# A two-layer hybrid transformer block on one core: the written order at the end of each mixer

## The chip, the cores and the metric

The kernel runs on one core of one Trainium2 chip. The time is the device time of one execution in microseconds (us), taken as the median of several runs. Names used below: TensorE (PE in rows; PEld its weight loads), VectorE (DVE), ScalarE (ACT), GpSimd (POOL) and SyncE (SP), which issues most loads and stores.

## What is computed

The reference runs 2 layers over 512 latent tokens (`x`) and 256 context tokens (`xc`) of width 1024, in fp32. Cut to one layer:

```python
mod = silu(c) @ w_ada[l] + b_ada[l]          # shifts, scales, gates; modc likewise
y, yc = _hybrid_mixer((x * (1 + sc1) + sh1) @ w_in[l], ...)
x = _layer_norm(ALPHA * x + g1 * (y @ w_out[l]), ln1_g[l], ln1_b[l])
x = _layer_norm(ALPHA * x + g2 * _swiglu(x * (1 + sc2) + sh2, w_ffn_in[l], w_ffn_out[l]), ln2_g[l], ln2_b[l])
if not last: ...the same two lines for xc, yc
```

`_hybrid_mixer` is an mLSTM, a differential attention and a grouped-query attention side by side; `_swiglu` is `(silu(u @ W_gate) * (u @ W_up)) @ w_out`. In the last layer only the 512 latent tokens go through the output projection, the norm and the feed-forward.

## The kernel before

**Tokens.** 768 tokens are six tiles of 128: T0, T1 context, T2 to T5 latent. Pairs are groups: 0 is (T0, T1), 1 is (T2, T3), 2 is (T4, T5). Layer 0 has all three at the end of its mixer, layer 1 only 1 and 2.

**Precision.** An fp32 matrix is held as a high and a low half (`wh`, `wl`; `tokh`, `tokl`), the high one a cast on ScalarE, the low one a subtraction on VectorE or POOL. `mm3` (L63) issues three matmuls for one product: high x high, low x high, high x low.

**The end of a mixer** (from L1039) is the output projection with the first layer norm, and the turn of its result into feature layout for the feed-forward. For each token tile T there are three steps:

- `first(c, T)`, c = 2 and 3: 21 matmuls of 256 columns (`pw<-wh,tokh` and so on), then two VectorE operations, L1045 and L1046, that add the result to the residual tile `rs`. (For c = 0 and 1 this was done earlier.)
- `second(T)`: the part of the projection that hangs on the mixer's last outputs, 6 matmuls of 512 columns into two PSUM tiles (`pw<-w`, source name `pw2`; PSUM, the accumulators that TensorE writes), then `finish`: VectorE L1085, L1088, L1089, L1090, L344, a power on POOL (`rstd`, L347), VectorE `nm` (L1156), and four ScalarE operations that normalise `rs` (L1094).
- `third(T)`: `to_feature` transposes the normalised tile on TensorE (8 x 128 columns, L266, `ptx<-ident,rs`, two PSUM tiles of four), ScalarE copies each 128 columns out with scale and bias (`v<-ptx`, L273, 8), casts twice to `tokh` (L275), and VectorE subtracts twice to `tokl` (L276).

`firsts(g)`, `seconds(g)` and `thirds(g)` do a pair of tiles. PSUM before `ps.pool.release()` is the mixer's pool; after it a pool of eight banks (`Banks`), with `pw2` in banks 2 and 3 and `ptx` in 4 and 5, each pair in rotation.

**The feed-forward's beginning.** `FfnA.load(fi)` (L1178) loads the gate and up columns of 128 hidden features and splits them (ScalarE `wh`, L293; VectorE or POOL `wl`, L294; with a pool given, L1192 and L1193). `FfnA.mm(fi, g)` (L1203) is the 48 matmuls of 256 columns of one feature block and one pair: `pc` for pair 0, `pg` and `pu` for the others, each in a bank of its own. Only two feature blocks, fi = 0 and 1, are given inside `mixer`; the rest follow in the feed-forward stage, where VectorE forms token and weight sums (`tf`, `tg`, L1231 to L1241; `S`, `wh`, `wy`, L1272 to L1293) for a scheme with fewer products, and, in layer 0, `aacc` sums of `w_ada` (L203, L205) for layer 1. `store_x1` (L1112) stores the normalised tiles for later.

**What sets the order.** The order is written by hand, but a scheduler of the language moves an instruction to another place in its engine's queue within what data and buffers allow; each engine then runs its queue in that order, and a waiting instruction holds all behind it.

Of the kernel before, what the change touches and what calls it, by code (L numbers as in the profile page):

```python
# [48 lines left out]
def kernel(ctx: ExitStack, tc: tile.TileContext, a: dict, out: bass.AP):  # L49
# [15 lines left out]
    def mm3(out, sh, sl, mh, ml, first, last):  # L65
        mm(out, sh, mh, first, False)
        mm(out, sh, ml, False, False)
        return mm(out, sl, mh, False, last)
# [188 lines left out]
    def tok_tiles(groups):  # L257
        return [{g: x[:, :, g * 256:(g + 1) * 256] for g in groups} for x in tokhl]
# [124 lines left out]
    def mixer(l, xh, xl, yd, ps, fill, pre):  # L383
        last = l == DEPTH - 1
# [7 lines left out]
        def pool(name, **kw):  # L392
            return tc.alloc_tile_pool(name=f"{name}{l}", reuse_waits="tile", **kw)
# [554 lines left out]
        ps = MixPS(f"psm{l}", acc=("acc", "pv"), q=("acc", "pv"))  # L948
# [18 lines left out]
        boost, fw, aw, pw, ow = MERGE[l]  # L967
# [4 lines left out]
        at = pool("at", bufs=2)  # L972
# [14 lines left out]
        groups = [1, 2] if last else [0, 1, 2]  # L987
# [49 lines left out]
        def first(c, T):  # L1037
            g, o = T // 2, (T % 2) * P
            cs = slice(c * 256, (c + 1) * 256)  # L1039
            wh, wl = W[c]  # L1040
            po = ps.tile([P, 512], F32, tag=("acc", "t")[T % 2], name="pw")[:, 0:256]
            for k in (0, 1, 6, 7, 2, 3, 4):
                mm3(po, Y[0][g][:, k, o:o + P], Y[1][g][:, k, o:o + P], wh[:, k, 0:256], wl[:, k, 0:256], k == 0, k == 4)
            r = R[c, T // 3][:, T % 3]
            V.tensor_tensor(po, po, rows["g1"][1 if T < 2 else 0][:, cs], ALU.mult)  # L1045
            V.scalar_tensor_tensor(r, r, ALPHA, po, ALU.mult, ALU.add)  # L1046
# [6 lines left out]
        xh, xl = {}, {}  # L1053

        anchor = [None]
        fa = FfnA(l)
# [12 lines left out]
        two = {"pw": pair, "tx": lambda: ps.tile([P, 512], F32, tag="t", name="ptx")}  # L1069

        def second(T):
            g, o = T // 2, (T % 2) * P
            pw = two["pw"]()
            for hf in range(2):
                mm3(pw[hf], yh[g][:, 5, o:o + P], yl[g][:, 5, o:o + P], w5[0][hf], w5[1][hf], True, True)
            with tc.issue_after(anchor[0].ins) if anchor[0] is not None else nullcontext():
                finish(T, pw)
# [18 lines left out]
        def third(T):  # L1096
            s, g = 1 if T < 2 else 0, T // 2
            if g not in xh:
                nh, nl = tok_tiles([g])
                xh.update(nh)  # L1100
                xl.update(nl)
            to_feature(lambda kk: R[kk // 2, T // 3][:, T % 3, (kk % 2) * P:(kk % 2) * P + P], T, xh, xl,
                       cols[(l, "ffn", s)], two["tx"],
                       lambda: at.tile([P, 4, P], F32, tag="og", name="v", bufs=3))
# [9 lines left out]
        def firsts(g):  # L1114
            for c in (2, 3):
                for T in (2 * g, 2 * g + 1):
                    first(c, T)

        def seconds(g):
            for T in (2 * g, 2 * g + 1):  # L1120
                second(T)

        def thirds(g):
            for T in (2 * g, 2 * g + 1):
                third(T)

        end = groups[-1]
        firsts(groups[0])
        for g in groups[1:]:
            if g == end:  # L1130
                fa.load(0, at)
            firsts(g)
            seconds(g - 1)
            thirds(g - 1)
        ps.pool.release()
        ps = fa.ps = Banks(f"psg{l}")
        two.update(pw=lambda: [ps.turn_of((2, 3), "pw2") for _ in range(2)], tx=lambda: ps.turn_of((4, 5), "ptx"))
        seconds(end)
        fa.load(1)
        for g in groups[:-1]:  # L1140
            fa.mm(0, g, xh, xl)
        thirds(end)
        fa.mm(0, end, xh, xl)
        for g in groups[:-1]:
            fa.mm(1, g, xh, xl)
        for i in range(2):
            store_x1(i)
        rows["pool"].release()
# [356 lines left out]
    ps = Banks("psm")  # L1505
# [5 lines left out]
    xh, xl = tok_tiles([0, 1, 2])  # L1511
# [82 lines left out]
    for l in range(DEPTH):  # L1594
        yd = tc.dram_tile([2, KD, P, NTOK], F32R, name=f"yd{l}")
        fill = [(0, 1), (0, 2)] if l == 0 else []
        xh, xl, ps, fa = mixer(l, xh, xl, yd, ps, fill, pre)
        nxt, pre, ps = ffn(l, xh, xl, ps, fa)
        if nxt:
            xh, xl = nxt  # L1600
# [37 lines left out]
```

## Time and profile before

| | |
|---|---|
| Time, median of 3 runs | 2044.14 us (2041.57 to 2046.82) |
| The profiled execution | 2053.77 us, its span 2052.0 us |
| Mean granted TensorE clock | 0.954 |
| TensorE matmul | 1905.9 us busy (93%), 12424 instructions |
| VectorE | 1369.3 us (67%) |
| ScalarE | 852.1 us (42%) |
| POOL | 341.5 us (17%) |
| Chain that ended last | TensorE 69%, VectorE 17%, DMA 5%, ScalarE 5% |

Over the span TensorE is the busiest engine by far, but its matmuls overlap and their ends are modelled, so 93% isn't a measure of how much could be won; what counts is where it stands still or runs at half clock. The ends of the two mixers lie at about 610 to 660 us (layer 0) and 1660 to 1705 us (layer 1).

### The profile page before, as it was taken

The numbers are of one execution on the slowest core, as the hardware profiler recorded it, in microseconds if no ns is written. First come the engines' busy times: TensorE is split into PE (matmuls) and PEld (weight loads), VectorE is DVE, ScalarE is ACT, GpSimd is POOL, SyncE is SP. The second block draws the span as 40 slices with busy tenths as digits, with TensorE's granted clock in tenths as the row PEclk, the third lists the DMA queues.
The fourth block names the chain that finished last, engine by engine and source line by source line (L and its number), as shares of the span: only waits on it lengthen the run. The fifth ranks groups of instructions, "written<-read, shape, count | busy, mean of one in ns | idle before, by whom it ended". The sixth has DMA issues, their size and how long they took to land.

```text
span 2052.0 us, 31613 instructions
## 1 busy us (share of the span) xinstructions
PE 1905.9 (93%) x12424; PEld 1695.6 (83%) x12424; DVE 1369.3 (67%) x2526; ACT 852.1 (42%) x1605; POOL 341.5 (17%) x287
## 2 busy tenths in 40 slices
PE   7889799999998999999699998879999989999998
PEld 5778767778987999999587788878889879999886
DVE  3556645576566999975556765755575578888746
ACT  4334355344346333433234433335553354444430
POOL 0223200112220000000301211421012610000301
PEclk9998899999998999999899999889999889999999
DMA  8211252226314446743665630121114333333431
GB/s 293 64 45 37 68 158 68 94 77 190 103 53 144 134 147 197 220 135 103 222 217 173 185 129 24 42 62 31 42 32 108 95 96 101 90 99 104 176 122 62
DMA packets 213232, 233.09 MB, mean 114 GB/s; under 512 B 14096, under 2 KB 185506, under 8 KB 213082
## 3 DMA queue, kind: packets, MB, share of 16 engines
q1 hardware_dynamic: 203034, 214.28, 33.6%
q0 software_dynamic: 10048, 16.78, 3.0%
q8 instruction: 98, 1.61, 0.3%
q14 instruction: 52, 0.43, 0.1%
HBM read 204.77 MB, written 26.25 MB: 113 GB/s over the span
## 4 chain that ended last, share of the span: by engine, by line
PE 69%; DVE 17%; DMA 5%; ACT 5%; issue 4%; SPq 1%; POOL 0%; DVEq 0%; ACTq 0%; POOLq 0%
PE po L63 18%; PE pacc L63 13%; PE px L1301 7%; PE pw L63 5%; PE pyz L1301 5%; PE s L63 5%; PE pv L63 3%; DMA raw<-w_ffn_in 3%; PE ppt L839 2%; DVE ca L455 2%; PE pg L63 1%; PE pu L63 1%; DMA araw<-w_ada 1%; DVE wl L1272 1%; PE pa L175 1%
## 5 line engine op out<-in xcount | busy, mean ns | idle before, releaser
L63 PE MATMUL po<-wh,tokh 128*128 128x256 f32 (+1 forms) x832 | 254.0, 305 | 10.7 <-DVE VG L418 3.5
L63 PE MATMUL po<-wh,tokl 128*128 128x256 f32 (+1 forms) x832 | 246.0, 296 | 0.0
L63 PE MATMUL po<-wl,tokh 128*128 128x256 f32 (+1 forms) x832 | 245.6, 295 | 0.0
L294 POOL TENSOR_TENSOR wl<-raw,wh 128x1024 fp32r<-128x1024 f32 x56 | 135.8, 2445 | 439.0 <-ACT wh L293 346.4
L63 PE MATMUL pacc<-wh,hh 128*128 128x512 f32 x440 | 173.9, 403 | 16.2 <-ACT hh L1434 15.2
L63 PEld LDWEIGHTS po<-wh,tokh 128*128 128x128 f32 x832 | 169.5, 204 | 21.5 <-issue 6.9
L63 PE MATMUL pacc<-wl,hh 128*128 128x512 f32 x440 | 176.1, 401 | 3.0 <-DVE wl L307 3.0
L63 PE MATMUL pacc<-wh,hl 128*128 128x512 f32 x440 | 172.2, 398 | 0.0
L63 PEld LDWEIGHTS po<-wl,tokh 128*128 128x128 f32 x832 | 169.8, 204 | 1.2 <-issue 0.2
L63 PEld LDWEIGHTS po<-wh,tokl 128*128 128x128 f32 x832 | 168.9, 203 | 1.1 <-issue 0.5
L826 DVE TENSOR_REDUCE mx<-s 128x1 f32<-128x768 f32 (+1 forms) x120 | 100.9, 848 | 48.0 <-PE s L63 47.5
L828 ACT ACTIVATE e<-s,mx 128x768 f32<-128x768 f32 (+1 forms) x120 | 98.0, 819 | 78.8 <-DVE mx L826 58.3
L63 PEld LDWEIGHTS pacc<-wh,hh 128*128 128x128 f32 x440 | 84.3, 192 | 39.1 <-ACT hh L1434 17.0
L307 DVE TENSOR_TENSOR wl<-raw,wh 128x1024 fp32r<-128x1024 f32 x66 | 97.9, 1515 | 25.8 <-ACT wh L306 25.6
L347 POOL TENSOR_TENSOR rstd<-rstd,nhalf 128x4 f32<-128x4 f32 (+2 forms) x52 | 43.5, 839 | 377.9 <-DVE rstd L344 324.4
L63 PEld LDWEIGHTS pacc<-wl,hh 128*128 128x128 f32 x440 | 83.9, 191 | 23.9 <-DVE wl L307 3.7
L418 DVE TENSOR_TENSOR pl<-ppt,ph 128x512 fp32r<-128x512 f32 (+1 forms) x112 | 71.9, 650 | 47.2 <-ACT ph L417 46.9
L63 PEld LDWEIGHTS pacc<-wh,hl 128*128 128x128 f32 x440 | 83.3, 189 | 20.1
L293 ACT CAST wh<-raw 128x1024 fp32r<-128x1024 f32 x70 | 70.6, 1051 | 62.4 <-issue 19.4
L417 ACT CAST ph<-ppt 128x512 fp32r<-128x512 f32 (+1 forms) x112 | 61.4, 558 | 77.4 <-PE ppt L839 73.3
L63 PE MATMUL s<-KA,QA 64*128 64x256 f32 (+1 forms) x432 | 86.6, 369 | 5.5 <-ACT e L828 4.0
L63 PEld LDWEIGHTS s<-KA,QA 64*128 64x128 f32 x432 | 62.6, 196 | 30.6 <-ACT e L828 10.9
(444 smaller groups left out, 5428.0 us busy)
## 6 DMA issues: line engine op xcount, KB each, us to landing
raw<-w_ffn_in SPq DMA_DIRECT2D x176, 256.0 KB
araw<-w_ada SPq DMA_DIRECT2D x80, 512.0 KB
raw<-w_ffn_out SPq DMA_DIRECT2D x66, 512.0 KB
raw<-w_in SPq DMA_DIRECT2D x32, 512.0 KB
raw<-w_out SPq DMA_DIRECT2D x18, 512.0 KB
hd<-th POOLq DMA_DIRECT2D x22, 384.0 KB, 3.5
hr<-hd SPq DMA_DIRECT2D x22, 384.0 KB
araw<-w_ada SPq DMA_DIRECT2D x32, 256.0 KB
```

The lines of the kernel that those rows point to most:

```text
L63: return TE.matmul(out, lhsT, rhs, start=start, stop=stop)
L293: S.copy(h, raw[:, :, 0:n])
L294: wsub[0].tensor_tensor(wl[:, 4 * hf:4 * hf + 4, 0:n], raw[:, :, 0:n], f32(h), op=ALU.subtract)
L307: V.tensor_tensor(wl[:, i * wide:(i + 1) * wide], raw[:, 0:wide], f32(h), ALU.subtract)
L347: last_pow[0] = G.tensor_tensor(r, r, nhalf[:, 0:n], op=ALU.pow)
L417: S.copy(dh, src)
L418: V.tensor_tensor(dl, src, f32(dh), ALU.subtract)
L455: V.scalar_tensor_tensor(ca[:, b0:b0 + n], cr[:, b0 + t:b0 + t + n], cw[:, l, fi, t:t + 1], ca[:, b0:b0 + n], ALU.mult, ALU.add)
L826: V.tensor_reduce(mx, s[:, 0:nk], AX.X, ALU.min)
L828: S.activation(e[:, 0:nk], s[:, 0:nk], AF.Exp, bias=mx, scale=-1.0, accum_out=su)
L839: TE.transpose(pt[:, i * P:(i + 1) * P], e[:, kt * P:(kt + 1) * P], ident)
L1301: TE.matmul(po, w[:, u, k], x[v][:, k], start=start and k + i == 0, stop=stop and k == 3 and i == 2, skip_group_check=True)
```

## The change

The loop at the end of `mixer` is replaced by two orders written out, one for each layer; the switch to the `Banks` pool becomes a function `to_banks`. In layer 0 all projections are given first, broken by the `seconds` and `thirds` of pair 0; `seconds` of pair 1 comes after the switch of pools; `mm` of pairs 0 and 1 is given between the `thirds`. In layer 1 the `seconds` of pair 1 are given before the projections of the last pair, and the `seconds` of the last pair before the `thirds` of pair 1; both `mm` of pair 1 come ahead of the last `thirds`.

```diff
--- before.py
+++ after.py
@@ -1124,25 +1124,46 @@
             for T in (2 * g, 2 * g + 1):
                 third(T)
 
+        def to_banks():
+            nonlocal ps
+            ps.pool.release()
+            ps = fa.ps = Banks(f"psg{l}")
+            two.update(pw=lambda: [ps.turn_of((2, 3), "pw2") for _ in range(2)], tx=lambda: ps.turn_of((4, 5), "ptx"))
+
         end = groups[-1]
         firsts(groups[0])
-        for g in groups[1:]:
-            if g == end:
-                fa.load(0, at)
-            firsts(g)
-            seconds(g - 1)
-            thirds(g - 1)
-        ps.pool.release()
-        ps = fa.ps = Banks(f"psg{l}")
-        two.update(pw=lambda: [ps.turn_of((2, 3), "pw2") for _ in range(2)], tx=lambda: ps.turn_of((4, 5), "ptx"))
-        seconds(end)
-        fa.load(1)
-        for g in groups[:-1]:
-            fa.mm(0, g, xh, xl)
-        thirds(end)
-        fa.mm(0, end, xh, xl)
-        for g in groups[:-1]:
-            fa.mm(1, g, xh, xl)
+        if last:
+            seconds(groups[0])
+            fa.load(0, at)
+            firsts(end)
+            to_banks()
+            seconds(end)
+            thirds(groups[0])
+            fa.load(1)
+            fa.mm(0, 1, xh, xl)
+            fa.mm(1, 1, xh, xl)
+            thirds(end)
+            fa.mm(0, end, xh, xl)
+        else:
+            firsts(1)
+            seconds(0)
+            fa.load(0, at)
+            for T in (4, 5):
+                first(2, T)
+            thirds(0)
+            for T in (4, 5):
+                first(3, T)
+            to_banks()
+            seconds(1)
+            fa.mm(0, 0, xh, xl)
+            thirds(1)
+            fa.load(1)
+            seconds(end)
+            fa.mm(0, 1, xh, xl)
+            fa.mm(1, 0, xh, xl)
+            thirds(end)
+            fa.mm(1, 1, xh, xl)
+            fa.mm(0, end, xh, xl)
         for i in range(2):
             store_x1(i)
         rows["pool"].release()
```

What the scheduler makes of it, at three places.

ScalarE in layer 0, where pair 0's copies out of the transposes begin (`v<-ptx`, with the per-feature scale and bias `col_ffn`; `rs` is a normalise, `wh<-raw` a weight cast). Before:

```order
L273 ACTIVATE v<-ptx,col_ffn_5638 128x128 x4
L275 CAST tokh<-v 128x4x128
L273 ACTIVATE v<-ptx,col_ffn_5638 128x128 x8
L1094 ACTIVATE rs<-rs,nm,rstd 128x256 x4
L275 CAST tokh<-v 128x4x128
L273 ACTIVATE v<-ptx,col_ffn_5638 128x128 x4
L275 CAST tokh<-v 128x4x128
L293 CAST wh<-raw 128x1024 x2
L1094 ACTIVATE rs<-rs,nm,rstd 128x256 x4
```

Changed:

```order
L293 CAST wh<-raw 128x1024 x2
L273 ACTIVATE v<-ptx,col_ffn_5638 128x128 x8
L275 CAST tokh<-v 128x4x128
L273 ACTIVATE v<-ptx,col_ffn_5638 128x128 x4
L275 CAST tokh<-v 128x4x128
L273 ACTIVATE v<-ptx,col_ffn_5638 128x128 x4
L275 CAST tokh<-v 128x4x128 x2
L293 CAST wh<-raw 128x1024 x2
L1094 ACTIVATE rs<-rs,nm,rstd 128x256 x4
```

The two weight casts that stood between T1's copies and the next normalise now stand ahead of all copies.

TensorE in layer 0 at the end of the projections and pair 1's transposes (`pw<-wh` projection; `pw_...<-w_...` the six wide matmuls of a `second`). Before, from T5's last projection to T4's `second`:

```order
L63 MATMUL pw<-wh,tokl 128x256
L266 MATMUL ptx<-ident,rs 128x128 x16
L63 MATMUL pw_6845<-w_6311,tokh 128x512
L63 MATMUL pw_6845<-w_6313,tokh 128x512
L63 MATMUL pw_6845<-w_6311,tokl 128x512
L63 MATMUL pw_6846<-w_6312,tokh 128x512
L63 MATMUL pw_6846<-w_6314,tokh 128x512
L63 MATMUL pw_6846<-w_6312,tokl 128x512
L63 MATMUL pc<-tokh,w_6619 128x256
```

Changed, from T5's `second` to the first `pg` of pair 1:

```order
L63 MATMUL pw_6939<-w_6314,tokh 128x512
L63 MATMUL pw_6939<-w_6312,tokl 128x512
L266 MATMUL ptx<-ident,rs 128x128 x8
L63 MATMUL pg<-tokh,w_6571 128x256
L63 MATMUL pu<-tokh,w_6571 128x256
L63 MATMUL pg<-tokh,wh 128x256
L63 MATMUL pu<-tokh,wh 128x256
L266 MATMUL ptx<-ident,rs 128x128 x2
```

T3's eight transposes now stand behind both `second`s of pair 2 and directly ahead of the first `pg` and `pu` of its pair; before, both tiles' sixteen stood together ahead of those `second`s.

TensorE in layer 1. Before, from the last projection to the first `pg`:

```order
L63 MATMUL pw<-wh,tokl 128x256
L266 MATMUL ptx<-ident,rs 128x128 x16
L63 MATMUL pw_16536<-w_16204,tokh 128x512
L63 MATMUL pw_16536<-w_16206,tokh 128x512
L63 MATMUL pw_16536<-w_16204,tokl 128x512
L63 MATMUL pw_16537<-w_16205,tokh 128x512
L63 MATMUL pw_16537<-w_16207,tokh 128x512
L63 MATMUL pw_16537<-w_16205,tokl 128x512
L63 MATMUL pg<-tokh,w_16310 128x256
```

Changed, from the last matmul of T4's `second` (its other five stand directly ahead) to the first `pg`:

```order
L63 MATMUL pw_16491<-w_16207,tokl 128x512
L266 MATMUL ptx<-ident,rs 128x128 x8
L63 MATMUL pw_16520<-w_16206,tokh 128x512
L63 MATMUL pw_16520<-w_16208,tokh 128x512
L63 MATMUL pw_16520<-w_16206,tokl 128x512
L63 MATMUL pw_16521<-w_16207,tokh 128x512
L63 MATMUL pw_16521<-w_16209,tokh 128x512
L63 MATMUL pw_16521<-w_16207,tokl 128x512
L266 MATMUL ptx<-ident,rs 128x128 x12
L63 MATMUL pg<-tokh,w_16370 128x256
L63 MATMUL pu<-tokh,w_16370 128x256
L63 MATMUL pg<-tokh,wh 128x256
```

T4's `second` now stands ahead of T2's transposes and T5's between T2's and T3's; four transposes of T4 have come ahead of the first `pg`.

## Rows read from the trace of the kernel before

**Rows 1.** Stretch, us, busy PE, PEld, DVE, ACT, POOL, clock, DMA, GB/s; layer 0.
```profile
610.00:620.00 10.00, 8.10 (x52) 7.30 (x51) 8.74 (x26) 8.81 (x23) 1.08 (x2) 0.87 0.14 44
620.00:630.00 10.00, 6.32 (x44) 5.44 (x42) 7.45 (x12) 10.00 (x21) 0.00 (x0) 0.84 0.73 224
630.00:640.00 10.00, 6.44 (x31) 5.46 (x32) 6.86 (x14) 5.65 (x15) 0.00 (x0) 0.61 0.34 100
```

**Rows 2.** TensorE's waits, 610 to 645 us: in total, times, longest.
```profile
PE ptx L266 <- ACT v L273: 4.0, 3, 1.6
PE pw L63 <- ACT v L273: 3.4, 2, 2.7
PE ptx L266 <- DVE rs L1046: 1.7, 1, 1.7
```

**Rows 3.** TensorE timeline, layer 0: start, duration, instruction, [idle before].
```profile
619.02 0.41 PE L63 MATMUL pw<-wl,tokh 128*128 128x256 f32 x1
619.23 0.41 PE L63 MATMUL pw<-wh,tokl 128*128 128x256 f32 x1
...
637.40 0.41 PE L63 MATMUL pc<-tokh,w 128*128 128x256 f32 x1
```

**Rows 4.** Chain that ended last, 640 to 750 us: start, duration, piece.
```profile
642.45 2.38 PE pc L63 x20
...
650.52 0.87 PE ptx L266 x8
...
659.96 0.75 DVE aacc L203
...
747.00 2.38 PE px L1301 x12
```

**Rows 5.** VectorE timeline before the `aacc` sums, layer 0.
```profile
658.68 0.69 DVE L276 TENSOR_TENSOR tokl<-v,tokh 128x512 fp32r<-128x512 f32 x1 [2.94 <-ACT tokh L275]
659.29 1.41 DVE L203 TENSOR_SCALAR aacc<-araw,cT 128x1024 f32<-128x1024 f32 x2
```

**Rows 6.** TensorE timeline, layer 0, first wait after the plain matmuls.
```profile
715.59 0.41 PE L1301 MATMUL pyz<-t0h,wh 128*128 128x384 f32 x1 [3.75 <-DVE th L1387]
```

**Rows 7.** ScalarE timeline, layer 0.
```profile
621.63 2.01 ACT L293 CAST wh<-raw 128x1024 fp32r<-128x1024 f32 x2
...
659.04 0.62 ACT L275 CAST tokh<-v 128x512 fp32r<-128x512 f32 x1
```

**Rows 8.** The same stretches view for layer 1.
```profile
1660.00:1670.00 10.00, 7.20 (x58) 6.74 (x56) 9.44 (x22) 4.53 (x6) 1.47 (x1) 0.93 0.19 54
1670.00:1680.00 10.00, 4.37 (x16) 2.54 (x15) 5.83 (x14) 9.69 (x24) 0.56 (x1) 0.50 0.71 209
...
1700.00:1710.00 10.00, 10.00 (x87) 10.00 (x86) 9.97 (x11) 3.69 (x5) 0.00 (x0) 1.00 0.00 0
```

**Rows 9.** TensorE's waits, 1660 to 1705 us.
```profile
PE ptx L266 <- ACT rs L1094: 6.3, 2, 3.5
PE ptx L266 <- DVE rs L1046: 1.4, 1, 1.4
```

**Rows 10.** ScalarE timeline, layer 1.
```profile
1668.52 2.08 ACT L1094 ACTIVATE rs<-rs,nm,rstd 128x256 f32<-128x256 f32 x4 [1.02 <-DVE nm L1156]
...
1671.48 2.90 ACT L273 ACTIVATE v<-ptx,col_ffn 128x128 f32<-128x128 f32 x8
1674.24 1.16 ACT L275 CAST tokh<-v 128x512 fp32r<-128x512 f32 x2
```

**Rows 11.** VectorE timeline, layer 1, last projection.
```profile
1671.17 0.42 DVE L1046 SCALAR_TENSOR_TENSOR rs<-rs,pw 128x256 f32<-128x256 f32 x1
```

**Rows 12.** TensorE timeline, layer 1.
```profile
1669.17 1.18 PE L266 MATMUL ptx<-ident,rs 128*128 128x128 f32 x4 [2.80 <-ACT rs L1094]
...
1682.07 0.38 PE L63 MATMUL pg<-tokh,w 128*128 128x256 f32 x1
...
1698.09 0.39 PE L63 MATMUL pg<-tokh,wh 128*128 128x256 f32 x1 [1.16 <-ACT v L273]
```

## The prediction

> **What bounds the kernel now.** I read the table of engine time by stretches first, around the end of each mixer, then TensorE's waits there, then the rows of ScalarE and VectorE that end them, and last the chain of work that ended last, to see whether time lost there is lost to the program.
>
> Layer 0: from 610 to 640 us TensorE is busy 8.10, 6.32 and 6.44 of each 10 us and its granted clock is 0.87, 0.84 and 0.61 [rows 1]; on both sides it is at 10.00 and 1.00. Its waits sum to 4.0 + 3.4 + 1.7 = 9.1 us, all for copies out of PSUM on ScalarE (`v`) and VectorE [rows 2]. A 256-column matmul starts every 0.21 us there at half clock (619.02 to 619.23) [rows 3], against 2.38/20 = 0.119 us at full clock [rows 4]. The work between 612 and 637.40 us, where the first feed-forward matmul stands [rows 3], is 42 projection matmuls (5.0 us at 0.119), 12 of twice the width (2.9) and some 32 transposes (0.87/8 = 0.11 each [rows 4], 3.5), so about 11.4 us in 25.4: 14 us are lost, 9.1 in waits and 5 to the clock.
>
> After that TensorE has plain work and VectorE takes over: the chain runs on VectorE with the `aacc` sums from 659.96 us on and is back on TensorE at 747.00 [rows 4]. The sums stand behind the last `tokl` of tokens T4 and T5: VectorE had idled 2.94 us for T5's first `tokh` cast, and begins `aacc` at 659.29 [rows 5]. TensorE then waits 3.75 us for VectorE's `th` at 715.59 [rows 6]. So in layer 0 it is not the 14 us that count but **when the `tokh` of T5 is cast** (659.04 [rows 7]).
>
> Layer 1: TensorE is busy 7.20 and 4.37 of 10 us from 1660 to 1680, at clock 0.93 and 0.50, and from 1700 on 10.00 at clock 1.00 [rows 8]. Waits: 6.3 + 1.4 us at the transposes [rows 9] and 1.16 at a `pg` [rows 12]. As TensorE is full behind it, what is lost here is lost to the program.
>
> **The change part by part.** No instruction is added or dropped; only the order, PSUM banks and waits move. 0.3% (about what a measurement of this kernel can tell from no change) is 6.1 us. Durations are those of the profiled execution, 2053.77 us with a span of 2052.0; the median of the runs shown is 2044.14, 0.47% below, and the sum is put on that median.
>
> *SyncE and POOL.* The loads of `w_ffn_in` no longer queue behind the four `x1d` stores, and POOL's and VectorE's splits of them follow. No wait of TensorE in either stage ends on a load [rows 2, 9, 12], so I cost it at nothing; the cover is ScalarE's work ahead of the casts. Were it gone, a load would cost at most the wait it ends, none of which is here.
>
> *Layer 0, first half.* All projections but those of the last tile (21 matmuls) now come ahead of the first transposes, which start at about 613.0. ScalarE's order puts two `wh` casts ahead of T0's `v` groups; the pair costs 2.01 us [rows 7]. So `v` starts at 615.15, and 16 of them (2.76 per 8 [rows 10]) with three casts of 0.55 end at 621.7. TensorE holds both `ptx` banks until the third group of four is read, so the last 21 projection matmuls start at 619.85 and, at 0.21 falling to 0.119, end at 623.8. The pair T2's `pw2` follows (to 626.3), then 47 matmuls of mm(0, 0), 5.6 us, to 631.9. Before, these began at 637.4 [rows 3]; this is the gain that the change makes here.
>
> *Layer 0, second half.* It pays for that with T2 and T3: their norm ran beside the first half, and now begins only after all projections. T2's normalise comes at 633.7. From there ScalarE has for four tokens 4 x 2.0 (normalise) + 4 x 2.76 (`v`) + 8 x 0.55 = 23.4 us [rows 10], so it cannot end before 657.1, and it waits on the way: about 2 us for T2's transposes, and again where T3's come only after T4's and T5's `pw2` (642.8 to 643.6). The first `pg` needs the `tokh` of T3, which I lay at 647.15: TensorE waits 3.55 us with nothing else ahead of it in its order. I let the clock fall there, as it did in [rows 1] after waits of this size on the same copies: 15 matmuls at 0.21 in place of 0.119, 1.5 us. Then come 50 matmuls (7.4 us with those 15), T4's eight transposes, 30 matmuls, T5's transposes with nine more between, ending at 660.9, and one `v` group and cast: the last `tokh` at 663.7 against 659.04 [rows 7], `aacc` at 663.4 against 659.29. That is +4.1 us on VectorE's chain. TensorE has by then done 185 plain matmuls instead of 135 and ends its plain part some 2 us sooner, where it then waits longer for VectorE [rows 6]; a part of VectorE's queue (weights, `w_ada` sums) doesn't hang on the tokens. I take **+3.0**, with ends 0 (VectorE makes up all of it) and +4.1 (nothing).
>
> The Trainium skill's "TensorE: Matmul & The Clock Gate", section "Loop structure matters more than you think", names the copy out of PSUM as work that doesn't break the clock's warmth, and long waits for loads as what does. The rows speak against it: there is no wait for a load here and the clock is 0.61 [rows 1, 2]. By the page the clock terms of both layers would be nil, and the sum +3.4 in place of +6.5.
>
> *Layer 1.* Same until 1666.4. Then TensorE's order puts T4's `pw2` ahead of T2's transposes. Its second half waits for VectorE's `rs` at L1046 of the last projection (1671.17 [rows 11]), so T2's transposes start at 1673.0; before, they waited only for ScalarE's normalise of T2 and started at 1669.17 [rows 12]. T5's `pw2` waits for VectorE as well. ScalarE then has T2's eight `v`, T3's normalise (2.0), T3's `v`, T4's normalise put before T3's casts, and the second cast ends about 1685.1; the first `pg` starts there. Before, the first `pg` stood at 1682.07 [rows 12], so +3.0, of which 1.8 us is paid back, since T4's and T5's `pw2` and four transposes are done by then; the half clock of the longer stretch takes 1.6 back. T4's and T5's transposes come later too, behind two more waits for `v`, and the `pg` that waited 1.16 us at 1698.09 [rows 12] comes at about 1701.5: **+3.5**, carried on, as TensorE is full behind it. Ends: 0 (all paid back) and +6 (none of the work done early helps).
>
> **Sum:** +3.0 + 3.5 = +6.5 us: the profiled 2053.77 would become 2060.3, and the median 2044.14 becomes 2050.6. With the ends of the two terms, 2044 to 2054.
>
> **The rivals.**
> 1. *Clock holds.* If TensorE's clock stays full in the new stretches, 1.5 and 1.6 us fall away: +3.4, 2047.5, no change. For it: more work stands on end, 47 and 50 matmuls against 42 before. Against it: 0.61 and 0.50 with the same waits [rows 1, 8].
> 2. *ScalarE is fed without a gap (the other side).* The place is ScalarE from T2's normalise to T5's last cast. In layer 1 that took from 1668.52 to 1700.5, 32 us, for 23.4 + 1.0 (one `wh` cast) of work, so 7.5 us are idle. If the feed-forward matmuls cover every wait, the end comes 7.5 us sooner there, and 2 us sooner in layer 0 (657.1 against 659.04): -9.5, 2034.6, faster. The point that decides: the 6.1 us are reached when, beside the 2 us of layer 0, layer 1 gives 4.1, so when ScalarE's idle time there falls below 7.5 - 4.1 = 3.4 us. For it: TensorE's waits of 6.3 us for a normalise [rows 9] are at places where other matmuls now stand. The Trainium skill's "Perfetto Trace Analysis", section "Matmuls", asks for just that, independent groups rotating through banks so that reading one out overlaps the next; no row shows yet that it does here. Against it: the new order's own waits above.
> 3. *Hidden in layer 0.* The `aacc` sums wait for loads of `w_ada` and absorb the whole +4.1; then only layer 1 counts: +3.5, 2047.6, no change. It also covers the case that the scheduler's order leaves the stage as long as it was.
> 4. *Half clock all through.* If TensorE stays at half clock from 619 to 647 and from 1670 to 1701, the roughly 100 and 40 matmuls there cost 0.09 more each: 12.6 on top of 3.4, of which some third falls in waits, so +12, 2056.
>
> **How the numbers follow.** The forecast 0.42, and it straddles the bound at 6.1: 0.25 slower, 0.17 no change. Rivals 1 and 3 together 0.18: 0.14 no change, 0.02 on either side. Rival 2, 0.30: half of it lies by its full price, 0.26 faster and 0.04 no change. Rival 4, 0.10, slower. Sums: faster 0.28, no change 0.35, slower 0.37. Range: from 2034 (rival 2 in full) to 2058 (rival 4 and a little), with no more than 2 in 10 left out; the forecast's own is 2044 to 2054.
>
> **What would show it.** Right: in layer 0 a wait of TensorE of 3 to 4 us before the first `pg`, after T3's transposes; feed-forward `pc` matmuls by 627 us; `aacc` begun at 662 to 664; two `wh` casts before the first `v`. In layer 1 the first `pg` at about 1685, after T4's and T5's `pw2`, and that stage's end, where TensorE is at 10.00 again, later by 3 to 4 us. Wrong: `aacc` before 659, ScalarE without gaps from T2's normalise to T5's cast, or TensorE at clock 1.00 through both stages.

## The result: slower by 0.5%, and the profile after

The changed kernel takes 2058.73 us (median of 7 runs, 2053.51 to 2064.82) beside 2046.11 us of the kernel before on the same chip: ratio 1.0052, interval 1.0034 to 1.0070, so +10.6 us (+7 to +14; the two medians alone lie 12.6 apart). Its profiled execution took 2059.73 us, 1.0 above its median; that of the kernel before lay some 8 us above the median of these runs. So stages are compared from an instruction ahead of the change on, not by whole executions. A "shift" below is how much later an instruction starts than its twin before, less the shift at `prs`, a TensorE instruction ahead of the stage.

TensorE's timeline before: the mark ahead of layer 0's stage, and a matmul of the output half of the feed-forward behind it.

```profile
597.04 0.95 PE L63 MATMUL prs<-ones,sq 128*128 128x2 f32 x8
...
1008.17 0.79 PE L63 MATMUL pacc<-wh,hh 128*128 128x512 f32 x1 [15.24 <-ACT hh L1434]
```

The same two after:

```profile
592.86 0.95 PE L63 MATMUL prs<-ones,sq 128*128 128x2 f32 x8
...
1011.48 0.79 PE L63 MATMUL pacc<-wh,hh 128*128 128x512 f32 x1 [14.97 <-ACT hh L1455]
```

The first starts 4.2 us sooner than before and the second 3.3 later: layer 0's stage, read this way, has grown by **7.5 us**. The same reading in layer 1 (from `prs` at 1655 to the first `px` of the feed-forward) gives +6.0. In kernels of the experiments that leave a stage as it was, it shows 0.0 to -0.7 for layer 0, but +0.8 to +1.9 for layer 1. So it is good to 1 us in layer 0, and in layer 1 it stands 1 to 2 us too high: +0.8 to +1.9 there is no change, and the +6.0 is some 4 to 5.

Engines by stretches after (columns as in [rows 1]), which answer to [rows 1] and [rows 8]:

```profile
610.00:620.00 10.00, 6.78 (x33) 5.77 (x33) 5.03 (x6) 8.71 (x22) 0.00 (x0) 0.66 0.36 105
620.00:630.00 10.00, 9.02 (x65) 8.31 (x64) 8.40 (x19) 2.00 (x2) 0.54 (x1) 1.00 0.36 107
630.00:640.00 10.00, 10.00 (x75) 9.32 (x74) 9.26 (x26) 7.70 (x18) 0.54 (x1) 1.00 0.48 157
640.00:650.00 10.00, 6.63 (x44) 6.29 (x42) 5.84 (x18) 8.11 (x19) 1.83 (x3) 0.83 0.19 62
...
1670.00:1680.00 10.00, 5.50 (x15) 3.89 (x16) 9.79 (x25) 7.52 (x17) 0.56 (x1) 0.55 0.85 249
1680.00:1690.00 10.00, 6.56 (x29) 5.16 (x29) 6.78 (x20) 9.35 (x24) 1.10 (x2) 0.67 0.01 2
...
1700.00:1710.00 10.00, 8.11 (x54) 7.63 (x53) 4.28 (x6) 6.35 (x16) 0.00 (x0) 0.83 0.01 2
```

In layer 0 the hole of the stretch 620 to 640 is closed, as meant; the one at 610 is deeper (6.78 where 8.10 stood) and a new one stands at 640. In layer 1 the stretch from 1700 on, which was at 10.00 and clock 1.00, has fallen to 8.11 and 0.83.

TensorE's waits after, 605 to 750 us and, from the fifth line on, 1655 to 1715 us (total, times, longest), for [rows 2, 9]:

```profile
PE px L1322 <- ACT ab L1340: 6.0, 1, 6.0
PE pg L63 <- ACT tokh L275: 3.4, 1, 3.4
PE ptx L266 <- ACT v L273: 2.4, 2, 1.8
PE pu L63 <- DVE wl L294: 1.9, 1, 1.9
...
PE pw L63 <- DVE rs L1046: 4.6, 1, 4.6
PE ptx L266 <- ACT rs L1094: 2.3, 1, 2.3
```

The short waits at the transposes of layer 0 have shrunk from 9.1 us (with `pw`) to about 5, but two long ones follow: 3.4 us before the first `pg`, and 6.0 where 3.75 stood [rows 6]. The 1.9 us for a weight split (`wl`) fall at 683.69, behind the stage, and are new too. TensorE's timeline at those places, and at the last wait of layer 1 (which answers to the one at 1698.09, [rows 12]):

```profile
643.61 0.58 PE L63 MATMUL pg<-tokh,w 128*128 128x256 f32 x1 [3.37 <-ACT tokh L275]
643.99 0.41 PE L63 MATMUL pu<-tokh,w 128*128 128x256 f32 x1
644.20 0.41 PE L63 MATMUL pg<-tokh,wh 128*128 128x256 f32 x1
...
720.07 0.69 PE L1322 MATMUL px<-t1h,wh 128*128 128x384 f32 x1 [6.02 <-ACT ab L1340]
...
1686.73 0.58 PE L63 MATMUL pg<-tokh,w 128*128 128x256 f32 x1 [1.15 <-ACT tokh L275]
...
1702.62 0.66 PE L266 MATMUL ptx<-ident,rs 128*128 128x128 f32 x4 [1.16 <-ACT v L273]
1704.01 0.39 PE L63 MATMUL pg<-tokh,wh 128*128 128x256 f32 x1 [0.74 <-ACT v L273]
```

ScalarE after, layer 0's last cast [rows 7], and the idle time ahead of T4's copies, in layer 0 and then in layer 1:

```profile
630.04 2.08 ACT L1094 ACTIVATE rs<-rs,nm,rstd 128x256 f32<-128x256 f32 x4 [7.73 <-DVE nm L1177]
...
651.83 2.90 ACT L273 ACTIVATE v<-ptx,col_ffn 128x128 f32<-128x128 f32 x8 [3.13 <-PE ptx L266]
...
659.86 0.62 ACT L275 CAST tokh<-v 128x512 fp32r<-128x512 f32 x1
...
1701.06 2.90 ACT L273 ACTIVATE v<-ptx,col_ffn 128x128 f32<-128x128 f32 x8 [8.96 <-PE ptx L266]
```

VectorE before, where the `aacc` sums catch up with their loads, some microseconds behind [rows 5]:

```profile
667.72 1.28 DVE L205 SCALAR_TENSOR_TENSOR aacc<-araw,cT,aacc 128x1024 f32<-128x1024 f32 x1 [0.53 <-DMA araw<-w_ada]
668.92 1.75 DVE L1231 TENSOR_TENSOR tf<-tokh 128x1536 f32<-128x1536 f32 x1
```

And after, with the start of the sums:

```profile
660.11 1.41 DVE L203 TENSOR_SCALAR aacc<-araw,cT 128x1024 f32<-128x1024 f32 x2
...
670.17 1.28 DVE L205 SCALAR_TENSOR_TENSOR aacc<-araw,cT,aacc 128x1024 f32<-128x1024 f32 x1 [2.27 <-DMA araw<-w_ada]
671.37 1.75 DVE L1252 TENSOR_TENSOR tf<-tokh 128x1536 f32<-128x1536 f32 x1
```

With the 4.18 us of the mark added, `aacc` begins at 664.29 against 659.29: +5.0. The load of `w_ada` is then waited for 2.27 us where it was 0.53, and the token sum `tf` comes at 675.55 against 668.92: **+6.6**. VectorE made nothing up; it lost more. TensorE's long wait in the feed-forward, which ends on this chain, grew from 3.75 to 6.02 us.

### The profile page after: what moved, and what is told of

Read it like the earlier page. It is cut to its first block, busy times and chain, and to the rows that moved or that the text cites. A ratio compares the mean times of both kernels' runs of the same rounds, so it can differ in the third digit from the quotient of the medians.

```text
span 2058.0 us, 31619 instructions
## 1 busy us (share of the span) xinstructions
PE 1908.1 (93%) x12424; PEld 1695.3 (82%) x12424; DVE 1366.0 (66%) x2526; ACT 849.7 (41%) x1605; POOL 341.1 (17%) x287
## 4 chain that ended last, share of the span: by engine, by line
PE 71%; DVE 15%; DMA 6%; ACT 4%; issue 3%; SPq 0%; POOL 0%; DVEq 0%; ACTq 0%; POOLq 0%
PE po L63 17%; PE pacc L63 13%; PE px L1322 9%; PE pyz L1322 6%; PE pw L63 5%; PE s L63 5%; PE pv L63 3%; DMA raw<-w_ffn_in 3%; PE ppt L839 2%; DVE ca L455 2%; PE pg L63 2%; PE pu L63 1%; DMA araw<-w_ada 1%; PE pa L175 1%; DVE wl L1293 1%
```

## The experiments

Eleven kernels ran, on three chips, each in several rounds beside the kernel before on the same chip. Layer 0's order and layer 1's can be set apart, so each edit goes into one layer and the other keeps the order of before, unless said. Shifts in us, read as above; "cast" is the last `tokh` cast of T5 in layer 0; times are (ratio - 1) x 2046 us. The ratios aren't quotients of the medians; these would give -7.7 us in the last row.

| kernel | cast | layer 0 | layer 1 | time | ratio, interval |
|---|---|---|---|---|---|
| the change | +5.0 | +7.5 | +6.0 | +10.6 | 1.0052 (1.0034 to 1.0070) |
| layer 0 of it alone | +5.2 | +7.7 | - | +8.0 | 1.0039 (1.0024 to 1.0054) |
| layer 1 of it alone | - | 0.0 | +5.2 | +3.7 | 1.0018 (1.0005 to 1.0032) |
| layer 0, last transposes sooner | +1.7 | +2.7 | - | +6.8 | 1.0033 (1.0016 to 1.0049) |
| layer 1, T2's transposes first | - | -0.7 | +6.2 | +4.1 | 1.0020 (1.0005 to 1.0035) |
| layer 1, last transposes sooner | - | -0.4 | +1.9 | -0.6 | 0.9997 (0.9978 to 1.0016) |
| before, all `second`s sooner | +0.7 | -0.2 | - | +0.8 | 1.0004 (0.9987 to 1.0022) |
| before, splits on POOL | +1.8 | +1.2 | +3.2 | +6.1 | 1.0030 (1.0007 to 1.0053) |
| combined, splits on POOL | -1.3 | -1.1 | +0.9 | -3.7 | 0.9982 (0.9966 to 0.9998) |
| before, layer 0's cast late | +6.5 | +6.2 | +1.2 | +2.9 | 1.0014 (0.9996 to 1.0033) |
| before, banks first in layer 0 | -5.6 | -6.9 | +1.9 | -5.7 | 0.9972 (0.9956 to 0.9988) |
| combined, without POOL | -5.6 | -6.8 | +0.9 | -9.6 | 0.9953 (0.9934 to 0.9971) |

### One layer at a time

Layer 0's branch as in the change, with the loop of before in the other (the diff, cut, is against the change); and the reverse.

```diff
         if last:
-            seconds(groups[0])
...
+            for g in groups[1:]:
...
```

> The new order in layer 0 only; layer 1 as before. Theory (VectorE's chain of sums starts later because the last token's cast is later, and TensorE waits for it after its plain work): about +6 us against the kernel before (+4.5 to +8), some two thirds of the whole change. Rival (only layer 1 counts, since layer 0's stage is hidden behind the w_ada loads): within 2 us of before.

> The new order in layer 1 only; layer 0 as before. Theory (TensorE is full behind the stage, so its later first and second pg blocks are carried to the end): +3.5 to +5 us against the kernel before. Rival (the matmuls done ahead pay it back by the end of the plain part): within 2 us.

Measured +8.0 and +3.7; together 11.7 against 10.6 for both. So the loss is two losses, and layer 0's is the larger, by their middles about two to one (+5 to +11 and +1 to +7).

### Layer 0: the last pair's transposes sooner

```diff
             seconds(end)
+            thirds(end)
             fa.mm(0, 1, xh, xl)
             fa.mm(1, 0, xh, xl)
-            thirds(end)
             fa.mm(1, 1, xh, xl)
```

> Layer 0 of the change with the last pair's transposes given ahead of the feed-forward columns of pairs 1 and 0 (two lines exchanged); layer 1 as before. Theory (the time of T5's last cast decides, not TensorE's waits in the stage): T5's last cast some 5 us sooner than in the run with layer 0 alone, the aacc sums begun as much sooner, and the time 3 to 6 us below that run, so near the kernel before. Rival (what counts is TensorE's time lost in the stage): TensorE waits more for copies, since less work stands between the transposes, and the time is the same as or above the run with layer 0 alone.

T5's cast came 3.5 us sooner than in layer 0's run (+1.7 against +5.2) and the stage 5 us sooner by the profile, but the times moved from +8.0 to +6.8 only, with intervals that overlap widely. TensorE's other waits up to that stage's end stayed: 3.38 us before the first `pg`, at 648.68, and clock 0.83 from 645 to 655, as in the change. So in the profile 5 us of the stage went with the cast and not with that wait. The profiled execution paid 1.66 us later, in the output half (TensorE's timeline of this kernel):

```profile
1033.17 0.51 PE L63 MATMUL pacc<-wl,hh 128*128 128x512 f32 x1 [1.66 <-DVE wl L307]
```

That is not enough to make up the difference. By its time this run doesn't confirm that the late cast is the loss.

### Layer 1: T2's transposes ahead of the last pair's seconds

```diff
             to_banks()
+            thirds(groups[0])
             seconds(end)
-            thirds(groups[0])
             fa.load(1)
```

> Layer 1 of the change with the transposes of pair 1 given ahead of the second of the last pair (two lines exchanged); layer 0 as before. Theory (T4's second, waiting for VectorE's last projection step, holds T2's transposes back by about 4 us): T2's transposes start at their old place, and the time is 3 to 4 us below the run with layer 1 alone, within 1.5 us of the kernel before. Rival (the loss comes from the switch of banks and from the order of ScalarE's copies): no gain over the run with layer 1 alone.

No gain over layer 1's order alone (+4.1 against +3.7). TensorE's timeline of this kernel (its `prs` mark 6.5 us sooner than before):

```profile
1663.05 1.18 PE L266 MATMUL ptx<-ident,rs 128*128 128x128 f32 x4 [3.13 <-ACT rs L1094]
...
1675.31 0.39 PE L63 MATMUL pg<-tokh,w 128*128 128x256 f32 x1 [1.35 <-ACT tokh L275]
...
1692.94 0.66 PE L266 MATMUL ptx<-ident,rs 128*128 128x128 f32 x4 [1.16 <-ACT v L273]
1694.33 0.66 PE L266 MATMUL ptx<-ident,rs 128*128 128x128 f32 x4 [0.74 <-ACT v L273]
1696.24 0.58 PE L63 MATMUL pg<-tokh,wh 128*128 128x256 f32 x1 [1.26 <-ACT v L273]
```

T2's transposes are back at their old time (1663.05 + 6.5 = 1669.6 against 1669.17, [rows 12]) and the first `pg` at 1681.8 against 1682.07. Yet the stage is as late as in the change, for its end has three waits, 1.16 + 0.74 + 1.26 us, at the last pair's transposes, with half clock behind them. The order of T2's transposes is not the cause; the profile shows this for the place alone; the times, with their intervals, could hide a gain of some 3 us.

### Layer 1: the last pair's transposes sooner

From that came a new theory: the change gives all 96 matmuls of pair 1 first, so that the last sixteen transposes are given together behind them (in the change's trace ten of them stand there, in the last run's all sixteen), with nothing to run while ScalarE copies.

```diff
             fa.mm(0, 1, xh, xl)
+            thirds(end)
             fa.mm(1, 1, xh, xl)
-            thirds(end)
             fa.mm(0, end, xh, xl)
```

> Layer 1 of the change with the last pair's transposes given ahead of the second feed-forward block of pair 1 (two lines exchanged); layer 0 as before. Theory formed from the runs so far (layer 1's loss lies at the last pair's transposes, which stand together behind all matmuls of pair 1, with three waits of TensorE for copies and half clock behind them): the loss there, some 5.5 us in waits and clock against 1.4 before, falls to 2 or less, and the time is 3 to 4 us below the run with layer 1 alone. Rival (the prediction's reason, T4's second ahead of T2's transposes): that order is unchanged here, so no gain.

-0.6 us against before (-5 to +3), 4.3 below layer 1's order alone, with intervals that overlap a little. Engines by stretches in this kernel:

```profile
1680.00:1690.00 10.00, 8.85 (x56) 8.65 (x56) 2.83 (x7) 9.33 (x24) 0.55 (x1) 0.70 0.48 158
1690.00:1700.00 10.00, 10.00 (x87) 10.00 (x87) 8.35 (x10) 4.83 (x10) 0.00 (x0) 1.00 0.01 2
```

The waits behind the last transposes are gone and from 1690 on TensorE is at 10.00 and clock 1.00. This kernel keeps T4's `pw2` ahead of T2's transposes, with its wait of 4.57 us. The stage's shift is +1.9, as in kernels that leave layer 1 as it was. By the profile, then, layer 1's loss is the **place of `thirds(end)`**, and what else the change moves there costs nothing that these runs can tell; the times go the same way.

### Layer 0 of before, all seconds ahead of pair 1's transposes

Against the loop of before, with its last round written out (cut); what moves is `seconds(end)`.

```diff
+            firsts(end)
+            seconds(end - 1)
+            seconds(end)
+            thirds(end - 1)
             to_banks()
-            seconds(end)
```

> The kernel before, with one step moved in layer 0: the second of the last pair given ahead of pair 1's transposes. Theory (VectorE's chain starts with T5's last cast): that cast comes some 4 to 7 us sooner, the sums start as much sooner, and the time is 3 to 6 us below the kernel before. Rival (TensorE's own lost time at the transposes decides): TensorE's waits in the stage stay at 9 to 10 us and the time stays within 2 us of before.

No change (+0.8). ScalarE's timeline shows why the cast did not move:

```profile
646.96 2.90 ACT L273 ACTIVATE v<-ptx,col_ffn 128x128 f32<-128x128 f32 x8 [11.04 <-PE ptx L266]
```

The norms were ready, but T4's transposes still stood behind all feed-forward matmuls given before them, and TensorE waited 5.60 us in one piece before the first `pc`. So this didn't test the theory that the cast decides; a cast can only come sooner if the transposes do.

### The load splits on POOL

```diff
-        wsub[0] = V
+        wsub[0] = G
...
+        wsub[0] = V
         for i in range(2):
             store_x1(i)
```

> The kernel before, with the low halves of the feed-forward weights that are loaded at the end of a mixer made on GpSimd in place of VectorE (1.2 us each on VectorE, 2.4 on GpSimd). Theory (in layer 1 VectorE's four splits stand between the last projections' steps and the norm of T2 and T3, and TensorE waits for that norm): TensorE's first wait in layer 1, 2.8 us before, shrinks to 1 or less, the second and third too, and the time is 2 to 4 us below the kernel before. Rival (ScalarE's copies are the bound in the stage): within 1.5 us of before. In layer 0 no change is expected from either.

Slower by 6.1 us (+1 to +11). POOL's timeline of this kernel:

```profile
1668.16 2.35 POOL L294 TENSOR_TENSOR wl<-raw,wh 128x1024 fp32r<-128x1024 f32 x1
```

And VectorE's:

```profile
1668.30 3.28 DVE L294 TENSOR_TENSOR wl<-raw,wh 128x1024 fp32r<-128x1024 f32 x1
1671.51 0.15 DVE L1178 SCALAR_TENSOR_TENSOR nm<-mv,rstd 128x1 f32<-128x1 f32 x1
```

The same subtraction takes VectorE 1.22 us elsewhere (median of the ten with these operands in this kernel); the one that begins 0.14 us behind POOL's ends 1.07 us after POOL's end, at 1670.51. So VectorE did next to nothing while POOL's ran, `nm` came at 1671.51, and TensorE's wait for T2's normalise was 5.74 us instead of 2.80 [rows 12]. That is about half of the 6.1; where the rest went wasn't followed up. The Trainium skill's "SBUF — State Buffer", section "Who interferes with whom", says the same, that an operation of VectorE with two inputs in the on-chip memory blocks fully against one of GpSimd that reads there; here the trace agrees.

### A combined kernel

The splits on POOL, layer 1 with both edits above, and in layer 0 the switch of banks and both `second`s of the last pair ahead of pair 1's transposes, so that these mix with pair 0's matmuls.

```diff
+            firsts(end)
+            seconds(end - 1)
+            seconds(end)
             to_banks()
-            seconds(end)
+            thirds(end - 1)
```

> Three edits together: the splits on GpSimd; in layer 0 the second of the last pair ahead of pair 1's transposes, with these given after the switch of banks; in layer 1 the change with the transposes of each pair ahead of the next pair's second and of the second feed-forward block. If the terms of VectorE's chain and of TensorE's lost time both hold, it is faster than the kernel before by 4 to 10 us. Rival: each gain is taken back by a later wait, and the time is within 2 us of before.

-3.7 us: a little faster than the kernel before, and short of the 4 to 10 us expected. One subtraction of VectorE again took 3.29 us, in layer 1's stage. In layer 0's stage the two met the other way round. VectorE's timeline of this kernel:

```profile
623.91 1.21 DVE L294 TENSOR_TENSOR wl<-raw,wh 128x1024 fp32r<-128x1024 f32 x1
625.05 2.36 DVE L1176 SCALAR_TENSOR_TENSOR nm<-mv,rstd 128x1 f32<-128x1 f32 x1
```

And POOL's:

```profile
623.98 3.42 POOL L294 TENSOR_TENSOR wl<-raw,wh 128x1024 fp32r<-128x1024 f32 x1
```

VectorE began 0.07 us first and took its usual time; POOL's took 3.42 us instead of 2.35, and VectorE's next operation, `nm`, 2.36 instead of 0.15, up to POOL's end. So whichever began first here kept the other waiting.

### The late cast by itself

The loop of before, with one block of 48 feed-forward matmuls moved ahead of the last transposes.

```diff
+            fa.mm(1, 0, xh, xl)
             thirds(end)
             fa.mm(0, end, xh, xl)
-            for g in groups[:-1]:
-                fa.mm(1, g, xh, xl)
+            fa.mm(1, 1, xh, xl)
```

> The kernel before, with one change in layer 0: the 48 matmuls of the first pair's second feature block are given ahead of the last pair's transposes instead of behind them, so that T5's last cast and the aacc sums come 48 x 0.119 = 5.7 us later, with no new wait and no half clock on TensorE before that. Theory (the end of T5's cast sets the layer's end, nothing of it is made up): last tokh at about 664.7 in before's time, aacc at about 665, and the run +5 to +8 us slower than before. Rival (the change's loss in layer 0 is the wait and the half clock at the first matmuls of pair 1, and VectorE makes up a late cast): within 2 us of before.

TensorE's timeline of this kernel, the long wait that grew:

```profile
716.65 0.66 PE L1322 MATMUL pyz<-t0h,wh 128*128 128x384 f32 x1 [7.51 <-DVE th L1408]
```

The cast came 6.5 us later, TensorE's wait for VectorE doubled from 3.75 [rows 6] to 7.51 us, and the stage grew by 6.2 in the profile: the mechanism is there without the change's wait before the first `pg`. `aacc` began 6.5 us later and `tf` 6.6, and the wait for `w_ada` between them was 0.98 us, so beginning late doesn't by itself make that wait long. The times say +2.9 us (-0.8 to +6.8): between theory and rival, with both within reach of the interval.

### Banks first in layer 0 alone, and the combined kernel without POOL

The layer 0 edit of the combined kernel alone; then with both edits of layer 1, all splits as in the kernel before.

> The kernel before, in layer 0 alone with both seconds of the last pair and the switch of pools ahead of pair 1's transposes, so that these stand between the feed-forward matmuls of pair 0; the splits of the loads stay where they are. Theory: the last cast and aacc come no later than before (in the combined run 657.7 and 658.9 in before's time, against 659.04 and 659.29), so 0 to -2 us. Rival (given pair 0's matmuls early costs by itself, as in the change): +3 to +8.

> The combined kernel without the splits on POOL: layer 0 as in the run with the banks first, layer 1 with pair 1's transposes first and the last pair's transposes ahead of pair 1's second feature block. Theory (the splits on POOL cost 6 us wherever they stand): -6 to -10 us against before. Rival (they cost only beside before's order, at the first transposes of layer 1): -1 to -5, as the combined run's -3.7.

-5.7 and **-9.6 us**: the second is the fastest kernel here, 0.9953 (0.9934 to 0.9971) of before, and some 20 us below the change, by the two ratios to before. It is 5.9 us below the combined kernel with POOL, as its theory had it. Whether layer 1's edits add to layer 0's isn't shown: the intervals of the two overlap, their medians on the same chip are 2039.70 and 2041.08, and layer 1's shift is +0.9 beside +1.9 with layer 1 unchanged. The first did better than either theory said. ScalarE's timeline of the first, from T3's copies on:

```profile
634.77 2.92 ACT L273 ACTIVATE v<-ptx,col_ffn 128x128 f32<-128x128 f32 x8
...
638.55 2.98 ACT L273 ACTIVATE v<-ptx,col_ffn 128x128 f32<-128x128 f32 x8
...
645.74 2.90 ACT L273 ACTIVATE v<-ptx,col_ffn 128x128 f32<-128x128 f32 x8 [3.18 <-PE ptx L266]
648.49 1.18 ACT L275 CAST tokh<-v 128x512 fp32r<-128x512 f32 x2
```

T4's copies follow T3's casts at once, and only T5's wait, 3.18 us. The last cast (the second of the two in the last line) comes 5.6 us sooner than before in the shift, and the stage ends 6.9 sooner. VectorE's timeline:

```profile
643.28 1.41 DVE L203 TENSOR_SCALAR aacc<-araw,cT 128x1024 f32<-128x1024 f32 x2
...
659.14 1.75 DVE L1254 TENSOR_TENSOR tf<-tokh 128x1536 f32<-128x1536 f32 x1
```

Here the scheduler put the first `aacc` ahead of T5's cast, 11.6 us sooner than before in the shift, but `tf` moved by 5.3 only, as the cast did. So it is `tf`, the sum over the tokens, that carries the cast's delay; `aacc` stood behind the cast before, and doesn't have to.

## Why the prediction was right in direction and too small

Forecast +6.5 us, straddling the bound, with slower the likeliest of the three; measured +10.6 (+7 to +14). On the 2044.14 us that the forecast started from, the ratio gives 2054.8, inside its range; the median of the runs, 2058.73, lies 0.7 above it. +10.6 is also just above +10.1, the upper ends of the two terms together.

- **Layer 0, first half: right.** With the 4.2 us of the mark added, `v` began at 615.2 (foreseen 615.15), the start of the last projections at 620.0 (619.85) and `pc` at 627.0 (626.3). The copies' end is mis-summed: 615.15 with 16 copies and three casts is 622.3, not 621.7; two casts stand there, and it measured 621.9.
- **Layer 0, second half: right as a layout.** T2's normalise stood at 634.2 (foreseen 633.7), the first `pg` at 647.8 (647.15) after a wait of 3.37 us (3.55), with matmuls every 0.21 us behind it, and T5's last cast at 664.1 (663.7).
- **Layer 0, the sum: this step failed.** Of +4.1 us on VectorE's chain I took +3.0, since "a part of VectorE's queue doesn't hang on the tokens". The delay was +5.0 at `aacc`, +6.6 at `tf`, +7.5 at the end of the stage, and layer 0 alone cost +8.0 us (+5 to +11). The upper end of the term, "nothing made up", was itself too low, for three reasons. By [rows 5, 7] `aacc` starts 0.25 us behind the start of the last cast, so with the cast that I laid at 663.7 the delay was +4.7 and not +4.1. Behind it VectorE waited longer for `w_ada` (2.27 against 0.53 us), which I had not priced; why that load came later is open, as a cast just as late met a wait of 0.98 us in another run. And TensorE's plain part, which I let end some 2 us sooner, ended 2.7 later (its first `px` at 708.08, with the mark 712.26, against 709.57), with 2.3 us more of waiting behind it. Of the 2.5 us that are left to +7.5, about 0.7 is the longer half clock behind that wait: in the 5.3 us from 720.07 on TensorE began 17 matmuls of 384 columns, before 21 in the 5.3 us from 715.59 on, and 4 x 0.175 at full clock is 0.7. The rest wasn't followed up.
- **Loads at nothing:** in the two stages that held, but not behind them: the wait for `w_ada`, and 1.95 us of TensorE for a weight split of VectorE at 683.69, weren't in the sum.
- **Layer 1: right in size, wrong in reason.** +3.5 foreseen, +3.7 (+1 to +7) measured alone; the first `pg` stood at 1685.3 (foreseen 1685.1) and the `pg` behind the last copies at 1702.6 (1701.5). But the reason given first, T4's `second` ahead of T2's transposes, fell: taking it back brought nothing, and moving `thirds(end)` alone removed the loss in the profile. What I had named in a clause, T4's and T5's transposes coming later, was the whole of it there. So the size was luck.
- **Rival 1 (clock holds) fell**, at those places: the clock was 0.66, 0.83, 0.55, 0.67 and 0.83 in the stretches with waits, none of them for a load. The sum of +3.4 that I took from the Trainium skill's "TensorE: Matmul & The Clock Gate", section "Loop structure matters more than you think", lies outside the measurement's interval too; what speaks against that reading is the clock in these stretches, as the time missed by other terms as well. **Rival 4**, +12, came nearest in size but not in kind: from 620 to 640 us TensorE was at 10.00 or close to it and 1.00. **Rival 3 fell:** the `aacc` sums did not absorb the delay.
- **Rival 2 (ScalarE fed without a gap) fell.** Between T2's normalise and T5's last cast ScalarE idled 3.13 us before T4's copies in layer 0 and 8.96 in layer 1, where its last cast came 5.5 us later by the mark and not 7.5 sooner. That the last kernel gained 9.6 us and the rival's price was 9.5 is luck: by the profile it gained 6.8 in layer 0 (the rival: 2) and nothing in layer 1 that stands out (the rival: 7.5), and its ScalarE still idles 5.7 and 7.1 us there.

Open: how much of layer 0's loss in time is the late cast. The profiles go with it in all kernels of the table (cast +6.5, +5.2, +5.0, +1.7, -5.6 against stage +6.2, +7.7, +7.5, +2.7, -6.9), also where the wait and half clock before the first `pg` stayed (+2.7) and where they were not there (+6.2). The times agree for the sooner cast (-5.7), but two runs lie off in opposite directions: +2.9 (-0.8 to +6.8) where the profile says +6.2, within the interval, and +6.8 (+3 to +10) where it says +2.7. Both have a new wait in the output half, 1.66 us in the one and 2.29 in the other, so that doesn't tell them apart. What the wait before the first `pg` costs by itself isn't shown; no run took it away alone.

## What to carry to other kernels

When transposes feed an engine that copies them out, give them in small groups between independent matmuls; a block of matmuls put ahead of the last group moves the last cast by about its own length (48 matmuls, 5.7 us: cast +6.5, stage +6.2 in the profile), however well it fills TensorE. Find the last instruction that the next engine's queue waits for, and cost a reorder by when that one ends, with nothing taken off for work that "could" go ahead unless a row shows it ready. A wait that is closed in the middle of a stage is not a gain until the end of the stage has moved.

## What was not expected of the hardware

- A subtraction of VectorE took 3.28 us instead of 1.22 when POOL had begun one like it 0.14 us before, and POOL's took 3.42 instead of 2.35 when VectorE was 0.07 us ahead. Work moved to an idle POOL was not free here.
- Low busy time didn't always come with a low clock. In the kernel with the banks first TensorE was busy only half of one stretch, with single waits of 3.40 and 2.22 us around it, and kept its full clock, where [rows 8] shows 0.50 at a busy share like it:

```profile
620.00:630.00 10.00, 4.96 (x41) 4.55 (x39) 10.00 (x22) 7.47 (x13) 0.54 (x1) 1.00 0.39 111
630.00:640.00 10.00, 9.28 (x78) 9.08 (x79) 3.77 (x8) 10.00 (x27) 1.02 (x2) 1.00 0.96 291
```

What decides it was not tried.
